# Three pairs of up blocks (13, 16, 19) in two by two steps in the second half, in place of 13 and 17

## The chip, the cores and the metric

The kernel runs on one core of a Trainium2 chip. The metric is the device time of one execution in microseconds, as the median of several runs. The engines go by short names in the profile: PE is TensorE (matrix products), PEld its weight loads, DVE is VectorE, ACT is ScalarE, POOL is GpSimd, SP is SyncE, which here only issues DMAs.

## What is computed

One layer of a residual network on a sequence of 512 positions with 1024 channels: an input projection with a short gated convolution and a causal attention, a gated merge, and then a channel mixer. The change lies in the mixer:

```python
h = rms_norm(x, norm_ffn_g[l])
up = causal_dwconv(h @ w_up[l], conv_ffn_w[l])
a, b = jnp.split(up, 2, axis=-1)
x = x + (jax.nn.silu(a) * b) @ w_down[l]
return rms_norm(x, norm_f_g)
```

`w_up` has 2 x 2816 columns. The causal convolution has three taps along the sequence, with weights of its own for each channel.

## The kernel before

**Layout.** Activations lie with channels on the 128 partitions and the 512 positions along the free axis, cut into two halves of 256. Every product is kept near float32 by splitting both factors into a high part of a shorter type and the rest: wh·xh + wl·xh + wh·xl (`mm3`, `passes`), three matmuls of 128x256 for each half.

**Weight chunks.** All weights come as one list of chunks (`stream`, L176 to L198), in the order of use. For each chunk SyncE's queue loads a raw tile (`load`, L223; five buffers, `NRAW`), ScalarE writes the high part (L281), VectorE the rest (L285); high and low parts have two buffers each (L271). This is `split`. A chunk is split about one chunk ahead of its matmuls.

**Plain and two by two blocks.** Each of the 22 up blocks `j` gives a tile of `a` and one of `b`. I number the chunks `up2j` and `up2j+1` as blocks, and `j` as pair. In a plain pair (`block`, L971) each of the two is 8 x 3 x 2 = 48 matmuls. A pair named in `UPS` goes through `up_pair` (L1090) instead: two output tiles, two input tiles and two position halves make a two by two product, done with seven products where eight would be needed (`PROD`, L343). Such a pair takes its weights as two P chunks (the blocks themselves, 768 columns used) and two F chunks (sums of blocks, 1024 columns), 84 matmuls in all, into four PSUM banks, and five VectorE steps and one of ScalarE put the results together (L1100 to L1106). The forms of the activations that it needs (`tfh`, `tfl`) lie in the buffer `xf`.

**After a pair.** The tile is scaled by the norm (L1124, L1122), convolved (`taps`: one ScalarE step L617, two VectorE taps L618 and L621), `a` goes through silu (L1134) and the product a·b is made on GpSimd (L1137 for even `j`, L1144 for odd). Up to the last pair of `UPS` the scaling is done in place in PSUM; behind it, in the buffer `xg`, which takes over the place of `xf` and also receives the residual from DRAM (L1111).

**Work for the down product.** The down projection is done with the same seven products. For each odd `j` the four forms t1 to t4 (L1154 to L1159) and the high and low parts gh, gl (L1163, L1164) are put on a list `later` with a due chunk and a planned cost. `run_later` (L226) takes them off when a chunk is split, as long as a budget lasts: 1.7 us for an up chunk, 0.45 us for the P and F chunks of an up pair (L291), and it stops at the first due entry that doesn't fit. `glu` empties the list (`flush`, L1139) at the next odd `j`. `after_split` queues what is taken off behind that chunk's split on its engine.

**Sums of weights.** The F chunks are made on the way by DMAs in DRAM (`group`, L134): for each group of two chunks SyncE issues a copy, GpSimd an accumulating add, and this three times, each step resting on the one before. The list `todo` holds them in batches; within a batch the steps of its groups alternate. `ticks` (L245) says how many steps go out when a chunk is split.

**Order.** TensorE's, SyncE's and GpSimd's work around the change is pinned to program order (`keep`). On VectorE and ScalarE, program order is the preference, but an instruction whose inputs are ready may be placed ahead of one whose inputs aren't, when the program is built; the chip then runs each engine in that order.

Of the kernel before, what the change touches and what calls it, by code (L numbers as in the profile page):

```python
# [40 lines left out]
PHASES = ((0, 12), (12, NP))  # L41
# [11 lines left out]
)  # L53
GS = 2
NFF = len(STEPS[0]) + len(STEPS[1])
UPS = (3, 7, 13, 17)
NUP = NFF + 2 * (8 - GS)

PLAIN = [(m, k) for m in (6, 7) for k in range(*PHASES[1])]
PCUTS = (0, 4, 12, 20)  # L60
# [3 lines left out]
def block_kernel(ctx, tc, xT, vecs, wv, win, wmix, wo, wup, wst, wdp, outT):  # L64
# [53 lines left out]
    dsp = ctx.enter_context(tc.tile_pool(name="dsp", bufs=1, space=bass.MemoryType.DRAM))  # L118
    sums = {}
    groups = [[NFF + 2 * j, NFF + 2 * j + 1] for j in range(KB - GS)]  # L120
    ends = [0, 4, len(groups)]
    for (j0, j1), n0, n1 in zip(PHASES, (0, len(STEPS[0])), (len(STEPS[0]), NFF - 1)):
        groups += [[NUP + 2 * i, NUP + 2 * i + 1] for i, j in enumerate(UPS) if j0 <= j < j1]
        if j0:
            ends.append(len(groups))
        groups += [list(range(n, min(n + 2, n1))) for n in range(n0, n1, 2)]
        if not j0:
            ends += [ends[-1] + 4, len(groups)]
    groups.append([NFF - 1])
    ends += [len(groups) - 2, len(groups)]  # L130
    nstep = [len(d) for d in STEPS[0] + STEPS[1]] + [2] * (2 * (KB - GS) + 2 * len(UPS))
    todo = []

# [22 lines left out]
            add(f(6, 8), w(4, 6)),  # L156
        ]

    for i0, i1 in zip(ends, ends[1:]):
        todo += [op for ops in zip(*map(group, range(i0, i1))) for op in ops]  # L160

    def tick():
        if todo:
# [6 lines left out]
    def up_n(j):  # L170
        return [NUP + 2 * UPS.index(j) + d for d in range(2)]

# [13 lines left out]
    n = 0  # L186
    for ph, (j0, j1) in enumerate(PHASES):
        for j in range(j0, j1):
            if j in UPS:
                for m in up_n(j):  # L190
# [35 lines left out]
    def run_later(k, us):  # L226

        n = 0
        while n < len(later):
            if later[n][0] <= k and later[n][1] <= us + 0.1:  # L230
                us -= later[n][1]
                with after_split():
                    later.pop(n)[3]()
            elif later[n][0] <= k:
                return
            else:
                n += 1
# [7 lines left out]
    def ticks(nm):  # L245

        if nm[0] in "iw":
            return 1
        if nm[0] == "m":
            return 2  # L250
        if nm[0] == "u":
            n = int(nm[2:])
            return 2 if (n % 4 == 0 and n > 4) or (n >= 2 * PHASES[1][0] and n % 4 < 3) else 1
        return int(nm[0] == "F" and (int(nm[1:]) % 2 == 1 or int(nm[1:]) >= NUP))

    def split(hl=None):
# [6 lines left out]
        if k >= gs0:  # L263
            for _ in range(ticks(nm)):
                tick()
# [24 lines left out]
        parts.append((hi, lo))  # L290
        run_later(k, 0.45 if nm[0] in "PF" and int(nm[1:]) >= NUP else {"u": 1.7, "P": 1.6, "F": 0.75, "d": 0}.get(nm[0], 3.5))  # L291

# [445 lines left out]
    n = 4 * H  # L738
# [72 lines left out]
    n = len(units)  # L811
# [278 lines left out]
    def up_pair(j):  # L1090

        nonlocal xg, x1
        flush([("xf", q) for q in range(4)])
        p23, p45, p16, p7 = banks = [acc(f"us{j}{i}") for i in range(4)]
        pair(up_n(j), x1_form, banks)
        z = fp.tile([P, S], F32, tag="fu", name=f"uz{j}", bufs=3)
        u = fp.tile([P, S], F32, tag="fu", name=f"uu{j}", bufs=3)[:, : S // 2]
        lo, hi = halves
        with after_split():
            nc.scalar.activation(z[:, lo], p16[:, lo], AF.Copy)  # L1100
            nc.vector.tensor_add(z[:, hi], p16[:, hi], z[:, lo])
            nc.vector.tensor_add(u, p7[:, lo], z[:, hi])
            nc.vector.tensor_add(z[:, hi], p45[:, hi], z[:, hi])
            nc.vector.tensor_add(p23, p23, z)
            p45h = p45.rearrange(halves_of, h=2)
            nc.vector.tensor_add(p45h, p45h, u.unsqueeze(1).to_broadcast([P, 2, S // 2]))  # L1106
        if j == UPS[-1]:
            xg = xfp.tile([P, 4 * KB, 2 * P], F32, tag="xf", name="xg")
            x1 = xg[:, : 2 * KB].rearrange(whole, h=2)
            for a in range(0, KB, 4):  # L1110
                nc.gpsimd.dma_start(x1[:, a : a + 4, :], x1d[:, a : a + 4, :])  # L1111
        return p23, p45

    def up(j, rb2, pu=None):
        uu = []
        if j in UPS:
            pu = up_pair(j)
# [401 lines left out]
```

## Time and profile before

| | us |
|---|---|
| median of 3 runs | 692.53 |
| lowest, highest | 691.62, 692.86 |
| profiled execution | 691.91 |
| its span, first to last instruction | 690.1 |
| first half's up blocks, from the first matmul of block 0 | 338.30 |
| first half's down steps | 466.68 to 523.80 |
| second half's up blocks | 523.80 to 629.92 |
| second half's down steps | 629.92 to 665.62 |

The lower rows are places in the profiled execution, in us from its span's start, read from the chain of work that ended last. Rows of engines give the start, the length, the engine, the line of the kernel, the operation, the tiles (out<-in) and in brackets how long the engine stood idle before, and who ended it. In rows of stages, the busy time of PE, PEld, DVE, ACT and POOL follow each other with their counts, then TensorE's granted clock, the DMA share and GB/s.

### The profile page before, as it was taken

How to read it: one execution, taken by the hardware profiler on the slowest of the kernel's cores; microseconds unless marked ns; L12 is line 12 of the kernel's file. 1: busy time of each engine (PE TensorE's matmuls, PEld its weight loads, DVE VectorE, ACT ScalarE, POOL GpSimd, SP SyncE). 2: the span in 40 equal slices, each digit the busy share in tenths (PEclk: the TensorE clock that was granted, in tenths of full speed). 3: DMA queues.
4: the chain of work that ended last, by engine and by line, in shares of the span. 5: the costliest groups of instructions: out<-in, count | busy, mean ns of one | idle time of the engine just before them, and what ended most of it. 6: DMA issues, size and time to landing. Idle time of an engine off the chain costs nothing.

```text
span 690.1 us, 14688 instructions
## 1 busy us (share of the span) xinstructions
PE 681.7 (99%) x5928; PEld 679.9 (99%) x5928; DVE 542.5 (79%) x857; ACT 362.2 (52%) x578; POOL 182.3 (26%) x206
## 2 busy tenths in 40 slices
PE   9999999999999999999999999999999999999995
PEld 9999999999999999999999999999999999999995
DVE  6678777886687877768887988977665897988785
ACT  6575556554564544446654536545433455535663
POOL 5123745444021010233412123330122134230000
PEclk9999999999999999999999999999999999999998
DMA  8526957478489696878696768679799978753523
GB/s 308 196 86 218 204 148 172 102 185 168 127 224 284 208 266 186 250 248 268 202 201 172 181 161 232 149 175 229 218 300 301 277 175 214 233 162 119 178 77 122
DMA packets 64196, 136.75 MB, mean 198 GB/s; under 512 B 5728, under 2 KB 29280, under 8 KB 63872
## 3 DMA queue, kind: packets, MB, share of 16 engines
q1 hardware_dynamic: 43488, 103.89, 45.7%
q0 software_dynamic: 19920, 31.23, 25.9%
q8 instruction: 46, 0.75, 0.4%
q10 hardware_dynamic: 720, 0.69, 0.3%
q14 instruction: 22, 0.18, 0.1%
HBM read 129.44 MB, written 47.71 MB: 257 GB/s over the span
## 4 chain that ended last, share of the span: by engine, by line
PE 95%; DVE 2%; ACT 1%; issue 1%; ACTq 0%; DVEq 0%
PE p_up L314 22%; PE p_in L314 14%; PE dn L332 13%; PE gs L332 8%; PE p_up L332 7%; PE p_wo L314 6%; PE us L332 6%; PE yc L332 3%; PE ya L314 3%; PE pa L526 2%; PE pb L528 2%; PE p_g L314 2%; PE o L707 2%; PE tp L692 1%; PE pdB L314 1%; PE pdA L314 1%
## 5 line engine op out<-in xcount | busy, mean ns | idle before, releaser
L314 PE MATMUL p_in<-xf,wh_in 128*128 128x256 f32 x576 | 95.7, 278 | 0.0
L148 POOL DMA_DIRECT2D sum<-in_wst_dram x63 | 66.0, 1180 | 112.4 <-DMA sum<-sum 83.5
L314 PE MATMUL p_up<-x1h,wl_up 128*128 128x256 f32 x440 | 85.7, 276 | 0.0
L314 PE MATMUL p_up<-x1l,wh_up 128*128 128x256 f32 x440 | 85.7, 276 | 0.0
L314 PE MATMUL p_up<-x1h,wh_up 128*128 128x256 f32 x440 | 85.7, 276 | 0.0
L314 PEld LDWEIGHTS p_in<-xf,wh_in 128*128 128x128 f32 x576 | 80.4, 188 | 0.7
L281 ACT ACTIVATE wh_F<-raw_F 128x1024 fp32r<-128x1024 f32 (+1 forms) x40 | 42.0, 1051 | 63.6 <-PE ya L314 25.8
L285 DVE TENSOR_TENSOR wl_F<-raw_F,wh_F 128x1024 fp32r<-128x1024 f32 (+1 forms) x40 | 50.2, 1256 | 27.8 <-ACT wh_F L281 26.6
L314 PEld LDWEIGHTS p_up<-x1h,wl_up 128*128 128x128 f32 x440 | 66.3, 188 | 0.0
L314 PEld LDWEIGHTS p_up<-x1l,wh_up 128*128 128x128 f32 x440 | 66.2, 188 | 0.0
L314 PEld LDWEIGHTS p_up<-x1h,wh_up 128*128 128x128 f32 x440 | 66.2, 188 | 0.0
L314 PE MATMUL p_in<-xf,wl_in 128*128 128x256 f32 x288 | 56.6, 278 | 0.1
L285 DVE TENSOR_TENSOR wl_up<-raw_up,wh_up 128x1024 fp32r<-128x1024 f32 x36 | 44.7, 1242 | 11.6 <-ACT wh_up L281 11.5
L281 ACT ACTIVATE wh_P<-raw_P 128x768 fp32r<-128x768 f32 (+1 forms) x40 | 33.4, 834 | 38.5 <-PE p_up L314 16.8
L281 ACT ACTIVATE wh_up<-raw_up 128x1024 fp32r<-128x1024 f32 x36 | 38.0, 1055 | 25.5 <-PE p_up L314 16.6
L285 DVE TENSOR_TENSOR wl_P<-raw_P,wh_P 128x768 fp32r<-128x768 f32 (+1 forms) x40 | 38.3, 956 | 11.6 <-ACT wh_P L281 6.2
L314 PEld LDWEIGHTS p_in<-xf,wl_in 128*128 128x128 f32 x288 | 43.5, 188 | 0.3 <-DVE wl_in L285 0.3
L1137 POOL TENSOR_TENSOR ge<-fu,fu 128x512 f32<-128x512 f32 x11 | 22.2, 2015 | 72.4 <-DVE fu L621 49.1
L332 PE MATMUL dn<-gl,wh_F 128*128 128x256 f32 x156 | 36.4, 276 | 0.0
L332 PE MATMUL dn<-gh,wh_F 128*128 128x256 f32 x156 | 36.3, 276 | 0.0
L285 DVE TENSOR_TENSOR wl_in<-raw_in,wh_in 128x1024 fp32r<-128x1024 f32 x24 | 30.2, 1256 | 6.1 <-ACT wh_in L281 6.0
L332 PE MATMUL p_up<-x1h,wh_up 128*128 128x256 f32 x136 | 32.5, 276 | 0.0
(361 smaller groups left out, 2074.8 us busy)
## 6 DMA issues: line engine op xcount, KB each, us to landing
raw_F<-sum SPq DMA_DIRECT2D x39, 512.0 KB, 5.9
raw_up<-in_wup_dram SPq DMA_DIRECT2D x36, 512.0 KB, 4.1
raw_P<-in_wst_dram SPq DMA_DIRECT2D x39, 384.0 KB, 3.8
raw_in<-in_win_dram SPq DMA_DIRECT2D x24, 512.0 KB, 3.7
sum<-in_wst_dram POOLq DMA_DIRECT2D x39, 256.0 KB, 6.4
sum<-in_wst_dram SPq DMA_DIRECT2D x19, 512.0 KB, 8.2
sum<-in_wst_dram POOLq DMA_DIRECT2D x19, 512.0 KB, 8.4
sum<-sum SPq DMA_DIRECT2D x38, 256.0 KB, 4.1
```

The source lines that it names most:

```text
L148: return lambda: keep(nc.gpsimd.dma_start(dst, src, accum_op=ALU.add))
L281: ins = nc.scalar.activation(hi, raw, AF.Copy)
L285: ins = nc.vector.tensor_sub(lo, raw, hi.bitcast(F32))
L314: keep(nc.tensor.matmul(out[:, cs], w, x[:, cs], start=start and i == 0 and c == 0, stop=stop and i == 2 and c == len(cut) - 1,))
L332: keep(nc.tensor.matmul(out, wl if x == 1 else wh, xl if x == 2 else xh, start=opens and bk not in seen, stop=closes and bk not in left,))
L526: keep(nc.tensor.matmul(pa[t][:, :VW], xt, w[:, :VW], start=start, stop=stop))
L528: keep(nc.tensor.matmul(pb[t], xt, w[:, VW:], start=start and t % 2 == 0, stop=stop and t % 2 == 1))
L692: keep(nc.tensor.transpose(tp[:, ks], pt[:, ks], ident))
L707: keep(nc.tensor.matmul(o[:, os_], vv[:, kb, pr, e, :], x[:, kb, cs], start=e == 0 and kb == 0 and i == 0, stop=e == 1 and kb == nk - 1 an ...
L1137: keep(nc.gpsimd.tensor_mul(ge, a.rearrange(halves_of, h=2), b.rearrange(halves_of, h=2)))
```

## The change

The second half's pairs in two by two steps are now 13, 16 and 19; 17 becomes a plain pair. That adds one group of weight sums, six DMA steps, to the 126 there were. The batches are written out as a tuple. More steps go out per chunk: two instead of one at wo2, wo4 and wo6 and at up10, up18 and up22. Since the scaling in PSUM goes up to the last pair of `UPS`, blocks 36 to 39 are now scaled there too, and the load of the residual follows pair 19.

```diff
-UPS = (3, 7, 13, 17)
+UPS = (3, 7, 13, 16, 19)
 NUP = NFF + 2 * (8 - GS)
+MIXED = (4, 2, 4, 4, 2, 4, 2)
...
     groups = [[NFF + 2 * j, NFF + 2 * j + 1] for j in range(KB - GS)]
-    ends = [0, 4, len(groups)]
     for (j0, j1), n0, n1 in zip(PHASES, (0, len(STEPS[0])), (len(STEPS[0]), NFF - 1)):
         groups += [[NUP + 2 * i, NUP + 2 * i + 1] for i, j in enumerate(UPS) if j0 <= j < j1]
-        if j0:
-            ends.append(len(groups))
         groups += [list(range(n, min(n + 2, n1))) for n in range(n0, n1, 2)]
-        if not j0:
-            ends += [ends[-1] + 4, len(groups)]
     groups.append([NFF - 1])
-    ends += [len(groups) - 2, len(groups)]
...
-    for i0, i1 in zip(ends, ends[1:]):
-        todo += [op for ops in zip(*map(group, range(i0, i1))) for op in ops]
+    i0 = 0
+    for n in MIXED:
+        todo += [op for ops in zip(*map(group, range(i0, i0 + n))) for op in ops]
+        i0 += n
+    assert i0 == len(groups)
...
         if nm[0] in "iw":
-            return 1
+            return 2 if nm in ("wo2", "wo4", "wo6") else 1
...
         if nm[0] == "u":
             n = int(nm[2:])
-            return 2 if (n % 4 == 0 and n > 4) or (n >= 2 * PHASES[1][0] and n % 4 < 3) else 1
+            return 2 if n > 4 and n % (4 if n >= 2 * PHASES[1][0] else 2) != (3 if n >= 2 * PHASES[1][0] else 1) else 1
```

Before, the batches held 4, 2, 4, 4, 2, 3 and 2 groups; now 4, 2, 4, 4, 2, 4 and 2, and the one group of pair 19 leads the sixth.

## The prediction

> **What bounds the kernel now.** I read the page first (shares of busy time, chain of work that ended last), then the chain in order of time around one pair of up blocks, then the busy time by stage, and last the order of VectorE's instructions there.
>
> ```profile
> span 690.1 us, 14688 instructions
> PE 681.7 (99%) x5928; PEld 679.9 (99%) x5928; DVE 542.5 (79%) x857; ACT 362.2 (52%) x578; POOL 182.3 (26%) x206
> PE 95%; DVE 2%; ACT 1%; issue 1%; ACTq 0%; DVEq 0%
> ```
>
> TensorE carries 95% of the chain and is never far from busy. A shorter list of matmuls is worth its full time, as long as nothing else takes TensorE's place. The chain in order of time (start, length, what, matmuls) shows the pace:
>
> ```profile
> 565.96 1.36 PE p_up L332 x12
> 567.32 4.08 PE p_up L314 x36
> ...
> 576.84 9.57 PE us L332 x84
> 586.40 1.36 PE p_up L332 x12
> ...
> 597.28 1.36 PE p_up L332 x12
> ```
>
> A plain block is 48 matmuls in 1.36 + 4.08 = 5.44 us, so 0.1133 us each, and blocks follow without a gap. A pair in two by two steps (the rows "us") is 84 matmuls: 84 x 0.1133 = 9.52, and pair 17 took 9.57, so 0.05 us was lost in it. Next, who is close behind TensorE: the stages between pair 13 and the down steps (us, then busy time per engine).
>
> ```profile
> 534.68:544.20 9.52, 9.52 (x86) 9.52 (x86) 7.49 (x7) 5.37 (x6) 1.43 (x2) 1.00 1.08 281
> 544.20:576.84 32.64, 32.64 (x290) 32.64 (x290) 29.38 (x44) 13.91 (x21) 11.02 (x9) 1.00 0.74 192
> 576.84:586.40 9.56, 9.56 (x86) 9.56 (x86) 7.54 (x10) 7.32 (x11) 3.80 (x3) 1.00 1.02 267
> 586.40:629.92 43.52, 43.52 (x387) 43.52 (x386) 39.67 (x60) 21.30 (x32) 12.09 (x10) 1.00 0.59 176
> ```
>
> The third column of busy times is VectorE: 7.49 + 29.38 + 7.54 + 39.67 = 84.08 of 95.24 us, 88%. It is the second bound of just this stage. ScalarE and GpSimd have room (47.90 and 28.34 by the same sums).
>
> **The change part by part. TensorE:** pair 19 becomes a two by two pair, 2 x 5.44 = 10.88 us out, 9.52 in: **-1.36 us**. Pair 16 takes the place of pair 17, which moves work and saves nothing. That is the whole gain, 0.20% of 692.53.
>
> **VectorE's sum.** Four splits for a pair in place of two, five combining steps more; the groups of splits by line (count | busy, mean ns | idle before, and its causes),
>
> ```profile
> L285 DVE TENSOR_TENSOR wl_up<-raw_up,wh_up 128x1024 fp32r<-128x1024 f32 x36 | 44.7, 1242 | 11.6 <-ACT wh_up L281 11.5
> L285 DVE TENSOR_TENSOR wl_F<-raw_F,wh_F 128x1024 fp32r<-128x1024 f32 (+1 forms) x40 | 50.2, 1256 | 27.8 <-ACT wh_F L281 26.6 <-DMA raw_up<-in_wup_dram 0.9 <-issue 0.2
> L285 DVE TENSOR_TENSOR wl_P<-raw_P,wh_P 128x768 fp32r<-128x768 f32 (+1 forms) x40 | 38.3, 956 | 11.6 <-ACT wh_P L281 6.2 <-PE gs L332 5.5
> ```
>
> and VectorE's instructions around pair 17's end in order of time (start, length):
>
> ```profile
> 584.14 1.25 DVE L285 TENSOR_TENSOR wl_up<-raw_up,wh_up 128x1024 fp32r<-128x1024 f32 x1 [0.99 <-ACT wh_up L281]
> 585.30 0.68 DVE L1164 TENSOR_TENSOR gl<-ge,gh 128x512 fp32r<-128x512 f32 x1
> 585.91 1.89 DVE L1164 TENSOR_TENSOR gl<-go,gh 128x512 fp32r<-128x512 f32 x3
> 587.72 0.41 DVE L1101 TENSOR_TENSOR uz<-us,uz 128x256 f32<-128x256 f32 x1
> 588.05 1.21 DVE L285 TENSOR_TENSOR wl_up<-raw_up,wh_up 128x1024 fp32r<-128x1024 f32 x1
> ...
> 591.29 0.69 DVE L1124 TENSOR_TENSOR us<-us,rb_n 128x512 f32<-128x512 f32 x1
> 591.89 0.69 DVE L1122 SCALAR_TENSOR_TENSOR us<-us,rb_n 128x512 f32<-128x512 f32 x1
> 592.49 0.68 DVE L1124 TENSOR_TENSOR xg<-p_up,rb_n 128x512 f32<-128x512 f32 x1
> 593.09 0.74 DVE L618 SCALAR_TENSOR_TENSOR fu<-us,vec,fu 128x511 f32<-128x511 f32 x1
> 593.75 1.23 DVE L285 TENSOR_TENSOR wl_up<-raw_up,wh_up 128x1024 fp32r<-128x1024 f32 x1
> 594.89 0.74 DVE L621 SCALAR_TENSOR_TENSOR fu<-us,vec,fu 128x510 f32<-128x510 f32 x1
> ...
> 601.96 1.21 DVE L285 TENSOR_TENSOR wl_up<-raw_up,wh_up 128x1024 fp32r<-128x1024 f32 x1
> ```
>
> Splits: 2 x 0.956 + 2 x 1.256 - 2 x 1.242 = 1.94 us. Combining runs from 587.72 to 591.29 with one split of 1.14 in it: 2.4 us. The stage then asks 84.08 + 4.3 = 88.4 us of VectorE in 95.24 - 1.36 = 93.9 us, 94%. On average it fits; the question is where the work falls. From start to start, in these rows, a multiply costs 0.60, a tap 0.66, a split 1.14 and a step of gl 0.60 (585.30 to 587.72 is 2.42 for four).
>
> **VectorE's deadline.** Pair 16 is followed by blocks 34, 35, 36 as pair 17 was by 36, 37, 38. A block's first eight matmuls (12 in the chain's piece, of which four are the low part) need only the high half; the low half must be there 8 x 0.1133 = 0.91 us after the block's start. For the third block after a split that began at 584.14, that is 597.28 + 0.91 = 598.19: **14.05 us**. What stands ahead of that split in program order, in before: two splits and itself 3.42, gl of pair 15 2.42, combining 2.4, three multiplies 1.80, six taps 3.96: 14.0 us. It fitted with nothing to spare. Program order didn't decide, though: the split at 593.75 overtook five taps and ended at 594.98, 3.2 us early. Its successor of 601.96 ended 603.17, against 597.28 + 5.44 + 0.91 = 603.63: 0.46 us in hand.
>
> After the change there is one thing more in that window. Pair 15's steps t1 to t4 (0.85 us by the planner's costs, twice) ran here, in a hole between plain blocks:
>
> ```profile
> 570.21 0.42 DVE L1154 TENSOR_TENSOR go<-ge 128x256 f32<-128x256 f32 x1
> ...
> 572.76 0.43 DVE L1155 TENSOR_TENSOR go<-go,ge 128x256 f32<-128x256 f32 x1 [1.48 <-POOL go L1144]
> 573.10 0.42 DVE L1158 SCALAR_TENSOR_TENSOR go<-go 128x256 f32<-128x256 f32 x1
> 573.56 0.42 DVE L1159 SCALAR_TENSOR_TENSOR go<-go 128x256 f32<-128x256 f32 x1
> 573.90 0.69 DVE L1124 TENSOR_TENSOR p_up<-p_up,rb_n 128x512 f32<-128x512 f32 x1
> ```
>
> The last three take 573.90 - 572.76 = 1.14 from start to start, the first another 0.34: 1.5 us. Pair 16 now begins where block 32 did (565.96), and its four chunks allow 0.45 us each, which 0.85 exceeds, so they wait for block 34: 14.0 + 1.5 = 15.5 us for 14.05, **1.4 us late**. Two of the four gl steps also come only when pair 17's product flushes the list, behind block 35's evacuation (0.60 + 2 x 0.66 = 1.92 more): 3.4 late at worst. At best the split overtakes as it did in before and the cost is 0. I take **2.2**, between 1.4 and 3.4, since the gl steps now lie ready in the hole that the split used at 593.75.
>
> **ScalarE at pair 16's first F chunk.** The F chunk is needed 18 x 0.1133 = 2.04 us into the pair. ScalarE's order at pair 17:
>
> ```profile
> 576.99 0.63 ACT L1134 ACTIVATE fu<-fu 128x512 f32<-128x512 f32 x1 [1.67 <-DVE fu L621]
> 577.52 1.04 ACT L281 ACTIVATE wh_F<-raw_F 128x1024 fp32r<-128x1024 f32 x1
> ```
>
> In before a silu that waited for VectorE stood ahead of it, and it ended at 577.52 + 1.04 = 578.56 for 576.84 + 2.04 = 578.88. With pair 15's silu in that place, and VectorE later by up to 1 us, it costs 0 to 1.2 us; I take 0.3, near the 0.05 that pair 17 lost.
>
> **Rest of the stage.** Time that VectorE stands idle inside a pair is no use to it, since the next chunk's buffer isn't free: 9.52 - 7.49 = 2.03 us in pair 13, 9.56 - 7.54 = 2.02 in pair 17. Three times that, 6.1 us, is more than the 93.9 - 88.4 = 5.5 left, so VectorE stays behind into the down steps: 0.6 us by this sum, 0 if the holes are filled, 2 if a pair's idle time is lost once more. I take 0.7.
>
> **Costed at nothing.** Scaling blocks 36 to 39 in PSUM rather than in xg (0.69 against 0.68 in the rows above). The load of x1 now follows pair 19; its first use in the sums of the down steps is some 40 us later, so I find no bill for it, 2 us of ScalarE at most if its copy of x1 waits. DMA and GpSimd: one group more is three copies and three adds, and pair 19 loads two P and two F chunks for two up chunks. First the adds as a group, then one row of GpSimd's order near the end of the output projection, the longest DMA time of the sums, and SyncE's wait for them (us in total, times, longest):
>
> ```profile
> L148 POOL DMA_DIRECT2D sum<-in_wst_dram x63 | 66.0, 1180 | 112.4 <-DMA sum<-sum 83.5 <-DMA sum<-in_wst_dram 28.6 <-issue 0.2
> ```
>
> ```profile
> 337.23 0.56 POOL L1021 DMA_DIRECT2D x1d<-xr  x1 [4.51 <-DVE xr L1015]
> ```
>
> ```profile
> sum<-in_wst_dram POOLq DMA_DIRECT2D x19, 512.0 KB, 8.4
> ```
>
> ```profile
> SPq L145 <- DMA sum<-in_wst_dram: 88.1, 21, 10.6
> ```
>
> 3 x 1.18 = 3.5 us of GpSimd fit its idle time. SyncE's queue stood up to 10.6 us behind one copy with weights queued after it, and in the split rows above only 0.9 us of VectorE's idle time ended with a weight load. Six more steps go out from wo2 to up22, so the steps for pair 19 end six chunks before its first F load. The first adds of the third batch now fall into wo6 and wo7, in GpSimd's queue ahead of the last x1 stores and square sums, on which the second norm waits: two adds, 2.4 us, against the 4.51 us that GpSimd idled there (0 to 2.4 if their copies land late; I take 0). Five buffers of 5.44 us cover a stop of 10.6; uncovered, it costs 0 to 4 us.
>
> [...] GpSimd and VectorE meet here, in the order of time of each:
>
> ```profile
> 539.46 1.29 POOL L1137 TENSOR_TENSOR ge<-fu,fu 128x512 f32<-128x512 f32 x1 [4.63 <-DVE fu L621]
> ```
>
> ```profile
> 539.66 2.16 DVE L285 TENSOR_TENSOR wl_F<-raw_F,wh_F 128x1024 fp32r<-128x1024 f32 x1 [0.44 <-ACT wh_F L281]
> ```
>
> The split took 2.16 instead of 1.23 us beside the product. [...]
>
> **The sum:** -1.36 + 2.2 + 0.3 + 0.7 = **+1.84 us** if all terms fall due; since a stall at block 36 lets VectorE catch up and takes from the last term, I forecast **+1.5 us**. The profiled execution took 691.91 (span 690.1), 0.62 under the median of 692.53; I add to the median: **694.0 us**.
>
> **Rivals. (a) VectorE's order hides all** (not slower): the split of block 36 overtakes, as its like did at 593.75. The second window then has these 1.5 us more, but pair 17's own t steps, which lay ahead of the split of 601.96, now follow it, so about 0.46 stays in hand: 692.53 - 1.36 = 691.2. For it: the overtaking in before; against: 94% load. **(b) VectorE in debt to the end:** 3.4 + 1.2 + 2.0 - 1.36 = +5.2: 697.7. For it: 100% busy stretches follow every pair. **(c) A stop of SyncE's queue** late in the ups: +2 after the saving: 694.5; against: 0.59 DMA share in the last stage. That fewer matmuls aren't issued at all can't be: the chunks of pair 19 say so.
>
> **How the numbers follow.** Forecast 0.46 (692.3 to 695.8), (a) 0.28, (b) 0.16, (c) 0.10. About 0.2%, 1.39 us, is what can be told from no change. Faster needs all of (a) and a little luck, half of it: 0.14. Slower is above 693.9: half the forecast, (b) and most of (c): 0.46. Same: 0.40. The range, 691.0 to 696.8, takes in (a) and leaves out the far ends of (b).
>
> **What would show it.** In the profile after: pair 19 as 84 matmuls in 9.5 us; a gap of 1.4 to 3.4 us in TensorE at block 36, the third after pair 16, ended by wl_up; t1 to t4 of pair 15 behind block 34's split. A chain without gaps would prove (a); a wait of wh or wl for a weight load, (c).

## The result and the profile after

| | before | after |
|---|---|---|
| median, us (10 runs each, taken together) | 692.38 | 694.96 |
| lowest, highest | 691.62, 693.76 | 693.45, 695.38 |
| profiled execution, and its span | 691.91, 690.1 | 693.69, 691.9 |

The ratio after to before is 1.0033, with a 95% interval of 1.0023 to 1.0042: the change costs 2.6 us by the medians. In the kernel after, helper lines stand two lower: the split is L279 and L283, matmuls are L312 and L330, the multiplies L1122 and L1120, the taps L616 and L619, t1 to t4 L1152 to L1157, gl L1162, silu L1132. The kernels of the experiments have line numbers of their own; there, go by the tiles. The page, first lines and chain:

```profile
span 691.9 us, 14692 instructions
PE 681.3 (98%) x5916; PEld 678.7 (98%) x5916; DVE 548.3 (79%) x864; ACT 364.5 (53%) x581; POOL 184.6 (27%) x209
PE 86%; DVE 8%; ACT 3%; issue 2%; DMA 1%; ACTq 0%; SPq 0%; DVEq 0%
```

Twelve matmuls fewer, as costed, and still TensorE's share of the chain fell from 95% to 86%: VectorE now carries 8%. The chain in order of time shows where it does, and that pair 19 runs at full pace:

```profile
589.25 1.14 DVE wl_up L283
590.43 0.75 PE p_up L330 x4
591.18 4.08 PE p_up L312 x36
...
600.70 9.52 PE us L330 x84
...
626.54 1.60 PE p_up L330 x12
...
632.31 1.37 PE dn L330 x12
633.69 1.05 ACT wh_F L279
634.79 33.95 PE dn L330 x297
668.74 6.80 PE pdA L312 x60
```

TensorE's waits by what ended them (us in total, times, longest):

```profile
PE p_up L330 <- DVE wl_up L283: 2.7, 1, 2.7
...
PE dn L330 <- ACT wh_F L279: 0.4, 1, 0.4
...
PE us L330 <- ACT wh_F L279: 0.2, 1, 0.2
```

The wait shown is less than what it costs, since the rows of matmuls overlap (0.28 us long here, 0.1133 from start to start). I measure the cost from start to start, less 0.1133 us for each matmul between. At block 36:

```profile
587.50 0.28 PE L330 MATMUL p_up<-x1l,wh_up 128*128 128x256 f32 x1
590.43 0.75 PE L330 MATMUL p_up<-x1h,wl_up 128*128 128x256 f32 x4 [2.65 <-DVE wl_up L283]
591.02 0.39 PE L312 MATMUL p_up<-x1h,wh_up 128*128 128x256 f32 x2
```

From 587.50 to 591.02 are 3.52 us for five matmuls, which take 0.57 at full pace: **2.95 us lost**. In the same way pair 16's first F chunk lost 0.45, block 43 0.25, and the first F chunk of the down steps 0.71; in before the up blocks and the down steps of the second half lost 0.05 in all. The sum is 4.36.

The books of the two profiled executions: the up blocks of the second half took 632.31 - 523.84 = 108.47 us against 106.12, that is +2.35 (= -1.36 + 0.45 + 2.95 + 0.25, and 0.06 in small pieces). The down steps took 36.43 against 35.70, +0.73. The rest, from the plain products to the end of the span, took 691.9 - 668.74 = 23.2 against 24.5, **-1.3**, which nobody had planned. Together +1.8, the difference of the spans. The medians differ by 2.6, though: of after's ten times, two lie at 693.45 and 693.69 (the profiled one) and eight at 694.85 to 695.38. So there are three things to explain: the gaps, the shorter end, and the second group of times.

### The profile page after: what moved, and what is told of

It is laid out like the page before. It is cut to its first block, busy times and chain, and to the rows that moved or that the text cites. A ratio compares the mean times of both kernels' runs of the same rounds, so it can differ in the third digit from the quotient of the medians.

```text
span 691.9 us, 14692 instructions
## 1 busy us (share of the span) xinstructions
PE 681.3 (98%) x5916; PEld 678.7 (98%) x5916; DVE 548.3 (79%) x864; ACT 364.5 (53%) x581; POOL 184.6 (27%) x209
## 4 chain that ended last, share of the span: by engine, by line
PE 86%; DVE 8%; ACT 3%; issue 2%; DMA 1%; ACTq 0%; SPq 0%; DVEq 0%
PE p_up L312 17%; PE p_in L312 14%; PE dn L330 13%; PE gs L330 8%; PE p_wo L312 6%; PE us L330 6%; PE p_up L330 5%; PE yc L330 3%; PE ya L312 3%; PE o L705 2%; PE pa L524 2%; PE pb L526 1%; PE tp L690 1%; PE pdB L312 1%; PE pdA L312 1%
## 5 line engine op out<-in xcount | busy, mean ns | idle before, releaser
L143 POOL DMA_DIRECT2D sum<-in_wst_dram x66 | 70.9, 1227 | 96.1 <-DMA sum<-sum 67.6
L312 PE MATMUL p_in<-xf,wh_in 128*128 128x256 f32 x576 | 95.7, 278 | 0.0
L312 PE MATMUL p_up<-x1h,wh_up 128*128 128x256 f32 x416 | 81.1, 276 | 0.0
L312 PEld LDWEIGHTS p_in<-xf,wh_in 128*128 128x128 f32 x576 | 80.4, 188 | 0.7
L312 PE MATMUL p_up<-x1h,wl_up 128*128 128x256 f32 x416 | 81.0, 276 | 0.0
L312 PE MATMUL p_up<-x1l,wh_up 128*128 128x256 f32 x416 | 81.0, 276 | 0.0
L279 ACT ACTIVATE wh_F<-raw_F 128x1024 fp32r<-128x1024 f32 (+1 forms) x42 | 44.2, 1052 | 65.0 <-PE ya L312 25.8
L283 DVE TENSOR_TENSOR wl_F<-raw_F,wh_F 128x1024 fp32r<-128x1024 f32 (+1 forms) x42 | 53.5, 1275 | 28.6 <-ACT wh_F L279 28.3
L312 PEld LDWEIGHTS p_up<-x1h,wh_up 128*128 128x128 f32 x416 | 62.7, 188 | 0.0
L312 PEld LDWEIGHTS p_up<-x1h,wl_up 128*128 128x128 f32 x416 | 62.6, 188 | 0.0
L312 PEld LDWEIGHTS p_up<-x1l,wh_up 128*128 128x128 f32 x416 | 62.6, 188 | 0.0
L312 PE MATMUL p_in<-xf,wl_in 128*128 128x256 f32 x288 | 56.6, 278 | 0.1
L279 ACT ACTIVATE wh_P<-raw_P 128x768 fp32r<-128x768 f32 (+1 forms) x42 | 35.1, 836 | 39.6 <-PE p_up L312 17.9
L279 ACT ACTIVATE wh_up<-raw_up 128x1024 fp32r<-128x1024 f32 x34 | 35.9, 1057 | 28.6 <-PE p_up L312 14.1
L283 DVE TENSOR_TENSOR wl_up<-raw_up,wh_up 128x1024 fp32r<-128x1024 f32 x34 | 42.3, 1244 | 9.5 <-ACT wh_up L279 9.4
L283 DVE TENSOR_TENSOR wl_P<-raw_P,wh_P 128x768 fp32r<-128x768 f32 (+1 forms) x42 | 40.1, 956 | 11.5 <-ACT wh_P L279 6.0
L312 PEld LDWEIGHTS p_in<-xf,wl_in 128*128 128x128 f32 x288 | 43.6, 188 | 0.3 <-DVE wl_in L283 0.3
L330 PE MATMUL dn<-gh,wh_F 128*128 128x256 f32 x156 | 36.5, 277 | 0.4 <-ACT wh_F L279 0.4
L330 PE MATMUL dn<-gl,wh_F 128*128 128x256 f32 x156 | 36.4, 276 | 0.0
L283 DVE TENSOR_TENSOR wl_in<-raw_in,wh_in 128x1024 fp32r<-128x1024 f32 x24 | 30.2, 1257 | 6.1 <-ACT wh_in L279 3.4
L1142 POOL TENSOR_TENSOR go<-fu,fu 128x512 f32<-128x512 f32 x9 | 12.6, 1396 | 72.9 <-DVE fu L619 54.5
```

Of the source, the lines that this page charges most:

```text
L143: return lambda: keep(nc.gpsimd.dma_start(dst, src, accum_op=ALU.add))
L279: ins = nc.scalar.activation(hi, raw, AF.Copy)
L283: ins = nc.vector.tensor_sub(lo, raw, hi.bitcast(F32))
L312: keep(nc.tensor.matmul(out[:, cs], w, x[:, cs], start=start and i == 0 and c == 0, stop=stop and i == 2 and c == len(cut) - 1,))
L330: keep(nc.tensor.matmul(out, wl if x == 1 else wh, xl if x == 2 else xh, start=opens and bk not in seen, stop=closes and bk not in left,))
L1142: return eng.tensor_mul(go[:, 0:2, :], a.rearrange(halves_of, h=2), b.rearrange(halves_of, h=2))
```

## The experiments

**1. The same kernel once more.**

> The kernel after once more, unchanged, for a second profile and more times. Of ten times two lay at 693.5 to 693.7 and eight at 694.9 to 695.4, and the profiled execution was one of the two. Theory (a gap of 2.7 us sometimes lets TensorE's granted clock fall, as the profiles of the denser schedule and of pair 16 in place of 17 showed behind gaps of 2.9 and 1.9 us): the times fall into the same two groups, and if the profiled execution is one of the upper group, its matmuls behind block 36's gap take 0.21 us in place of 0.113 for some 2.5 to 3 us, 1.2 to 1.7 us in all. Rival (the upper group has another cause, as a DMA that lands late): an upper execution shows full clock and a longer or a second gap.

Times 693.33 and 693.37, and 694.51 to 696.84 (four); 1.0039 of before, 1.0023 to 1.0054. The profiled execution, 694.71, was of the upper group. TensorE there, in order of time:

```profile
587.43 0.28 PE L330 MATMUL p_up<-x1l,wh_up 128*128 128x256 f32 x1
590.36 1.22 PE L330 MATMUL p_up<-x1h,wl_up 128*128 128x256 f32 x4 [2.65 <-DVE wl_up L283]
591.38 0.63 PE L312 MATMUL p_up<-x1h,wh_up 128*128 128x256 f32 x2
591.81 0.63 PE L312 MATMUL p_up<-x1h,wl_up 128*128 128x256 f32 x2
```

The gap is the same to the hundredth. Behind it two matmuls take 0.43 us (591.38 to 591.81) in place of 0.23, until 593.4. That is 1.3 us more, and the table by stage gives a granted clock of 0.68 for 590 to 595, where the first profile had 1.00. So the stall at block 36 is paid twice in most executions of this kernel: once as the wait (2.65 us), and once as the slow stretch behind it (1.3 us). The mean granted clock of the executions agrees: in the sixteen of both sets it is 0.997 to 0.998 in the four of the lower group and 0.994 to 0.996 in the other twelve. That explains the second group, but for the one time of 696.84, which lies 1.6 us above the others of its set.

**2. Pair 15's work earlier.** The last F chunk of pair 16 gets the budget of an up chunk, so t1 to t4 and gl of pair 15 don't wait for block 34.

```diff
-        run_later(k, 0.45 if ...
+        run_later(k, 1.7 if nm == f"F{NUP + 7}" else 0.45 if ...
```

> The kernel after, with the budget at the last F chunk of pair 16 at 1.7 us in place of 0.45, so that t1 to t4 of pair 15 (1.5 us) and its gl steps run inside pair 16 rather than behind block 34's split. Theory (the 1.5 us of t1 to t4 are what the window to block 36 could not take): the gap at block 36 is gone or under 0.5 us, the time about 692.3 (691.5 to 693.2). Rival 1 (VectorE's load, not this work's place): the gap stays at 2 us or more. Rival 2 (the work only moves): the gap goes and another of 1 us or more appears at blocks 34 or 35, whose splits now stand behind this work; time 693.5 to 695.

Median 691.47, ratio to before 0.9991 (0.9981 to 1.0001): 3.5 us under after by the medians, 2.9 by the two ratios to before. The gap at block 36 is gone; the losses at the first F chunks of pairs 16 and 19 and of the down steps and one at block 42 stay, 1.9 us in all. VectorE's order says why. First the kernel after, from block 34's split to block 36's:

```profile
573.72 1.25 DVE L283 TENSOR_TENSOR wl_up<-raw_up,wh_up 128x1024 fp32r<-128x1024 f32 x1 [0.98 <-ACT wh_up L279]
574.90 0.41 DVE L1152 TENSOR_TENSOR go<-ge 128x256 f32<-128x256 f32 x1
...
576.02 0.42 DVE L1157 SCALAR_TENSOR_TENSOR go<-go 128x256 f32<-128x256 f32 x1
576.36 1.22 DVE L283 TENSOR_TENSOR wl_up<-raw_up,wh_up 128x1024 fp32r<-128x1024 f32 x1
...
585.91 0.74 DVE L616 SCALAR_TENSOR_TENSOR fu<-p_up,vec,fu 128x511 f32<-128x511 f32 x1
586.57 1.42 DVE L1162 TENSOR_TENSOR gl<-go,gh 128x512 fp32r<-128x512 f32 x1
587.91 0.74 DVE L619 SCALAR_TENSOR_TENSOR fu<-p_up,vec,fu 128x510 f32<-128x510 f32 x1
588.57 0.68 DVE L1122 TENSOR_TENSOR p_up<-p_up,rb_n 128x512 f32<-128x512 f32 x1
589.16 1.21 DVE L283 TENSOR_TENSOR wl_up<-raw_up,wh_up 128x1024 fp32r<-128x1024 f32 x1
```

Then the kernel with the earlier budget, the same split of block 36:

```profile
574.06 0.41 DVE L1153 TENSOR_TENSOR go<-go,ge 128x256 f32<-128x256 f32 x1
...
583.98 1.21 DVE L283 TENSOR_TENSOR wl_up<-raw_up,wh_up 128x1024 fp32r<-128x1024 f32 x1
585.11 1.40 DVE L616 SCALAR_TENSOR_TENSOR fu<-us,vec,fu 128x511 f32<-128x511 f32 x2
```

In after the split comes at 589.16, behind six taps, the last gl and block 35's multiply. With t1 to t4 and the gl steps of pair 15 out of the way (1.5 us and one late gl) it comes at 583.98, ahead of the taps, as its like did at 593.75 before the change: 5.2 us earlier for some 3 us of work moved, since the split now overtakes.

**3. The splits placed ahead.**

```diff
             p = pu[s_] if pu else block(f"up{2 * j + s_}", x1h, x1l, True)
+            if j == 17 and len(parts) == chunk.n:
+                split()
```

> The kernel after, with one thing moved: in pair 17 the splits of blocks 35 and 36 are called ahead of the evacuations of blocks 34 and 35, so that in VectorE's order the split of block 36 stands ahead of the taps of pair 17. Theory (the split of block 36 stands too far back in VectorE's order): the gap of 2.7 us at block 36 is gone or under 0.5, VectorE's busy time in the stage is the same, and the time falls by 2 to 2.9 us to about 692.3. Rival (VectorE simply has too much to do behind pair 16, whatever its order): the gap goes to one of blocks 37 to 39 or to pair 19, in sum over 2 us, and the time stays at 694.5 to 695.

Median 693.89, ratio 1.0023 (1.0012 to 1.0035). Both theories hit and missed: blocks 34 to 37 run without a gap, but 2.49 us are now lost at block 42, the third after pair 19. VectorE's order there repeats the picture of block 36:

```profile
605.10 1.22 DVE L283 TENSOR_TENSOR wl_up<-raw_up,wh_up 128x1024 fp32r<-128x1024 f32 x1 [0.19 <-ACT wh_up L279]
606.24 0.42 DVE L1154 TENSOR_TENSOR go<-ge 128x256 f32<-128x256 f32 x1
...
614.63 1.21 DVE L283 TENSOR_TENSOR wl_up<-raw_up,wh_up 128x1024 fp32r<-128x1024 f32 x1
```

The t steps and gl of pair 17 now fall behind pair 19's first split. So the argument of the window holds there too, and a gap avoided at one pair was handed to the next.

**4. Pair 16 in place of 17, without a third pair** (`UPS = (3, 7, 13, 16)` in the kernel before).

> Before with pair 16 in two by two steps in place of 17, and no third pair: the number of matmuls is that of before. Theory (the stall comes from pair 16's place, right behind an odd plain pair): the gap of 2 to 3 us at block 36 and the one of 0.2 to 0.4 at pair 16's first F chunk are there as in the kernel after, and the time is 2.3 to 3.4 us over before, about 695.2. Rival (the debt of three pairs is what stalls): no gap over 0.5 us at block 36, time within 0.6 us of before.

Median 696.25, ratio 1.0053 (1.0040 to 1.0065). The place alone does it, without a third pair: 0.43 us at pair 16's first F chunk, 2.25 at block 36, and then a slow stretch of 1.7 us, in sum 4.4, with no matmul saved. I had not counted the slow stretch. VectorE just ahead of block 36's split:

```profile
586.55 0.69 DVE L1164 TENSOR_TENSOR gl<-go,gh 128x512 fp32r<-128x512 f32 x1
587.15 0.74 DVE L621 SCALAR_TENSOR_TENSOR fu<-xg,vec,fu 128x510 f32<-128x510 f32 x1
...
588.41 1.21 DVE L285 TENSOR_TENSOR wl_up<-raw_up,wh_up 128x1024 fp32r<-128x1024 f32 x1
```

It is the order of after, 0.75 us earlier, and all of that is one row: gl takes 0.60 from start to start here and 1.34 in after, where GpSimd made its product at the same time (in experiment 4 it made it only at 592.79):

```profile
586.15 1.29 POOL L1135 TENSOR_TENSOR ge<-fu,fu 128x512 f32<-128x512 f32 x1 [9.13 <-ACT fu L1132]
```

**5. Only the schedule of the sums** (after, with the pairs of before).

```diff
-UPS = (3, 7, 13, 16, 19)
+UPS = (3, 7, 13, 17)
-MIXED = (4, 2, 4, 4, 2, 4, 2)
+MIXED = (4, 2, 4, 4, 2, 3, 2)
```

> The pairs of before (13 and 17) with the batches and the steps per chunk of after: only the schedule of the sums of weights is that of the change. Theory (these DMAs cost nothing): within 0.4 us of before, 692.0 to 692.8, and TensorE without a gap over 0.3 us in the second half's up blocks. Rival (part of the loss comes from the denser sums): 0.6 us or more over before, with a wait on a DMA or on GpSimd behind wo2 to wo7 or up10, up18, up22.

Median 696.64, ratio 1.0062 (1.0043 to 1.0080): a clear miss. ScalarE and GpSimd behind pair 17:

```profile
594.09 0.72 ACT L615 ACTIVATE fu<-xg,vec 128x512 f32<-128x512 f32 x1
600.65 0.42 ACT L1343 ACTIVATE gh<-xg 128x256 fp32r<-128x256 f32 x1 [5.84 <-DMA xg<-x1d]
600.97 0.62 ACT L1132 ACTIVATE fu<-fu 128x512 f32<-128x512 f32 x1
```

```profile
588.67 0.81 POOL L143 DMA_DIRECT2D sum<-in_wst_dram  x1 [3.67 <-DMA sum<-sum]
589.19 1.44 POOL L1109 DMA_DIRECT2D xg<-x1d  x2
```

The load of x1 stands in GpSimd's queue behind an add that waited 3.67 us for its copy; before the change it went out at 586.71, here at 589.19. ScalarE has a small copy of x1 (L1343) in its order right behind pair 17, and stands at it for 5.84 us, against 1.97 in before, with pair 17's silu behind it. The same two rows in before:

```profile
586.71 1.16 POOL L1111 DMA_DIRECT2D xg<-x1d  x2 [0.75 <-PE us L332]
```

```profile
596.88 0.42 ACT L1345 ACTIVATE gh<-xg 128x256 fp32r<-128x256 f32 x1 [1.97 <-DMA xg<-x1d]
```

In the kernel with the denser sums a gap of 2.94 us at block 39 follows, and a slow stretch of 2.7 us.

**6. The same, with x1's copy late.** Only one of the last products uses the copy, some 80 us later (596.88 to 675.83 in before); the planner had put it early since it reckoned x1 to be there.

```diff
-    nc.scalar.activation(xlast[0], y7, AF.Copy)
-    nc.vector.tensor_sub(xlast[1], y7, xlast[0].bitcast(F32))
+    with after_split():
+        nc.scalar.activation(xlast[0], y7, AF.Copy)
+        nc.vector.tensor_sub(xlast[1], y7, xlast[0].bitcast(F32))
```

> The pairs of before with the schedule of sums of after, and the copy of x1 moved back in ScalarE's order to where it is used. With the copy early this schedule took 696.6. Theory (the denser sums cost only because x1 lands later and ScalarE stands at its copy, 5.8 us): no gap over 0.3 us in the second half's up blocks, full clock, 691.8 to 692.6 like before. Rival (the sums take something else, such as the transfers of weights): 694 or more, with the gap at block 39 still there and another wait ahead of it.

Median 691.58, ratio 0.9994 (0.9985 to 1.0003), without a gap behind pair 17. So the denser sums themselves cost nothing in the up blocks. The time isn't quite like before's for another reason: this kernel has the shorter end of experiment 9 (4.8 us for 5.9), and its last products come 0.3 us later. The price of the copy is therefore better taken against before, whose median in the set of experiment 5 was 691.93: one instruction of 0.42 us in a wrong place had cost 4.7 us.

**7. The same step on top of experiment 2.**

> The kernel with the budget of 1.7 us at pair 16's last F chunk, and besides it the copy of x1 that stands in ScalarE's order behind pair 19, 60 us before its use, moved back to where it is used. Theory (ScalarE stands 2.3 us at that copy until x1 has landed, and silu and the high parts behind it are late): ScalarE's wait for x1 goes, the gap of 0.38 us at block 42 shrinks or goes, and the gap at the first down step (0.78 us) too in part; 0.3 to 0.9 us under the kernel without this, about 690.9. Rival (VectorE alone is late there): the same gaps, time within 0.2 us of 691.5.

Median 691.49 (0.9995, 0.9986 to 1.0004) against 691.47: a miss. ScalarE's wait for x1 is gone and the loss at block 42 falls from 0.38 to under 0.2 us, but the down steps reach their first F chunk at 632.17 in both kernels. So with pair 19 last, that wait (2.53 us in after) costs nothing that shows.

**8. ScalarE's order at the F chunks.** In after, ScalarE at pair 16 and at the down steps:

```profile
566.58 0.64 ACT L1132 ACTIVATE fu<-fu 128x512 f32<-128x512 f32 x1 [3.25 <-DVE fu L619]
567.12 1.05 ACT L279 ACTIVATE wh_F<-raw_F 128x1024 fp32r<-128x1024 f32 x1
```

```profile
633.15 0.64 ACT L1132 ACTIVATE fu<-fu 128x512 f32<-128x512 f32 x1 [3.23 <-DVE fu L619]
633.69 1.04 ACT L279 ACTIVATE wh_F<-raw_F 128x1024 fp32r<-128x1024 f32 x1
```

ScalarE idles for a tap of VectorE with the high part queued behind. On top of experiment 7, the splits are called ahead of silu there, and silu is put behind them; the sum steps stay where they were, by lines that are left out here.

```diff
...
+        if j + 1 in (*UPS[-2:], PHASES[1][1]):
+            if j % 2:
+                flush()
+            split(now=False)
+            split(now=False)
+            with after_split():
+                nc.scalar.activation(a, a, AF.Silu)
+        else:
+            nc.scalar.activation(a, a, AF.Silu)
```

> The kernel with pair 15's work early and x1's copy late, and besides it ScalarE's high parts of the first F chunk of pair 16, of pair 19 and of the down steps ahead of the silu that waited for VectorE's tap there; VectorE's order is unchanged. Theory (what is left of the loss are these three places: 0.43, 0.27 and 0.71 us against the pace of 0.1133 us per matmul): all three under 0.1, time 1.2 to 1.5 us under the kernel without this, about 690.1. Rival (VectorE's low parts or the later products then stall TensorE at the blocks behind): two or more gaps of 0.3 us elsewhere, time 691 or more.

Median 689.91, ratio to before **0.9967 (0.9956 to 0.9978)**: faster than both kernels, by 2.2 and 5 us. ScalarE and the chain now:

```profile
565.95 1.06 ACT L284 ACTIVATE wh_F<-raw_F 128x1024 fp32r<-128x1024 f32 x1 [2.76 <-PE p_up L317]
...
567.64 0.62 ACT L1143 ACTIVATE fu<-fu 128x512 f32<-128x512 f32 x1
```

```profile
565.87 9.52 PE us L335 x84
...
624.01 0.74 PE p_up L335 x4
...
628.83 35.26 PE dn L335 x311
```

The high part starts with the pair, and the three places are free of loss. VectorE's 864 instructions stand in the same order as in experiment 7, and of ScalarE's 581 only the three silu steps moved, so ScalarE's order alone was the cause there. Only block 42 still loses 0.41, to the low part that VectorE made at 622.75. Of the 2.2 us under before, 1.3 are the shorter end (4.6 us for 5.9, see experiment 9), and TensorE's part is 1.36 - 0.41 = 0.95.

**9. The shorter end.** From the issue of the last output copies to the end of the span it is 5.9 us in before (684.22 to 690.1) and 4.6 in after (687.34 to 691.9). Three kernels, each the one before with something idle added: five copies on SyncE's queue, six small copies on VectorE, six on ScalarE.

> Before with five short copies more on SyncE's queue (their data is not used), as many DMAs as the third pair brings there. From the issue of the last output copies to the end of the span it is 5.9 us in all kernels with two pairs, 4.6 in all with three, and the queue of instruction loads shows 22 loads against 23. Theory (the shorter end comes from where SyncE's program is loaded, not from the third pair's work): the end is 4.6 us, 23 loads, and the time is 1.0 to 1.4 us under before, about 690.8. Rival (the end depends on the work or its data): 5.9 us, time as before or up to 0.5 over it.

> Before with six copies of one column on VectorE more (their data is not used). Five copies more on SyncE's queue had left the end of the span at 5.7 us behind the issue of the last output copies. In all runs so far the end is 5.7 to 5.9 us where VectorE's program has 1090 instructions and ScalarE's at most 847, and 4.6 to 4.8 where VectorE's has 1091 or more and ScalarE's 848 or more. Theory (VectorE's program length decides, by where its last load of instructions falls): the end is 4.6 to 4.8 us, the time 0.8 to 1.3 us under before, about 691.0. Rival (ScalarE's): 5.7 to 5.9 us, time as before.

> Before with six copies of one column on ScalarE more (their data is not used), the counterpart to the six on VectorE. Theory (VectorE's program length decides over the end): 5.7 to 5.9 us from the last issue to the end, time as before or up to 0.3 over it. Rival (ScalarE's does): 4.6 to 4.8 us, 0.8 to 1.3 under before. If both kernels have the long end, neither length is the cause.

The copies on SyncE's queue changed nothing: 5.7 us, 1.0008 (0.9999 to 1.0017). The times of the other two can't be compared with before. They took 703.01 and 703.82 (1.0158 and 1.0169), with no wait that accounts for it: both have a new tile of 24 bytes per partition, and a block took 1.42 + 4.25 = 5.67 us for 5.44. Their ends can be compared with each other, though, since their matmuls end within 0.04 us: with the six on VectorE the end is 5.2 us (696.02 to 701.2), with the six on ScalarE 6.0 (696.06 to 702.1). That speaks for VectorE's program and against ScalarE's. Hence once more, with six copies of an old tile onto itself:

```diff
+            if j == 5:
+                with after_split():
+                    for i in range(6):
+                        nc.vector.tensor_copy(tbl, tbl)
```

> Before with six copies more on VectorE again, this time of a small tile onto itself, so that no new tile moves the others in SBUF (with a new tile of 24 bytes per partition each matmul took 0.1163 us in place of 0.1133, and the question of the end was not answered). Theory (the length of VectorE's program, 1096 instructions for 1090, decides where its last instructions are loaded): matmuls at 0.1133 us, the end 4.6 to 4.8 us behind the issue of the last output copies in place of 5.9, time 0.8 to 1.3 us under before, about 691.0. Rival (it has another cause): the end is 5.7 to 5.9 us, time as before or up to 0.3 over it; then the cause of the shorter end stays open.

Median 691.05, ratio 0.9990 (0.9981 to 0.9999). The issue of the last copies, in before and in this kernel, whose spans are 690.1 and 689.2:

```profile
684.22 1.63 ACTq L1383 DMA_DIRECT2D out_dram<-xg  x2
```

```profile
684.36 1.63 ACTq L1387 DMA_DIRECT2D out_dram<-xg  x2
```

The end is 4.8 us for 5.9, with six instructions that do nothing. The change brings VectorE eight more (1098 for 1090, counted in the trace), and the end with them. All fourteen profiles fall in line: 5.7 to 6.0 us with 1090 instructions on VectorE, 4.8 to 5.2 with 1091 or 1096, and 4.6 with 1098 or more. That the end goes with the length of VectorE's program is shown by these; that it works through the loading of its last instructions is a guess of mine that no run shows. The count of loads that I had named doesn't follow: it stays at 22 here and is 23 in after.

## Why the prediction was right

The forecast was +1.5 us and slower, +2.6 came, inside the range. Point by point:

- **TensorE, -1.36:** right. Pair 19 is 84 matmuls in 9.52 us.
- **VectorE's sum, 88.4 us:** right. The stages from pair 13 to the down steps in the table by stage (sum of us, then busy time per engine) give 88.31:

```profile
sum 97.59, PE 94.76 PEld 94.21 DVE 88.31 ACT 49.22 POOL 29.91; mean PE 15.79 PEld 15.70 DVE 14.72 ACT 8.20 POOL 4.99
```

- **The deadline at block 36:** the mechanism was right and the size short, 2.2 against 2.95. From 573.72 to the split's end at 590.37 VectorE worked without a hole for 16.65 us. Counted were 15.5; block 35's multiply (588.57) adds 0.6, as part of the worst case had it, and the one slow gl 0.74, together 0.2 more than measured. Of the two gl steps that the worst case had behind the rest, one came late. The prediction has a split that took 2.16 us beside a product of GpSimd; here it was a gl step that took longer, 1.34 us from start to start beside the product and 0.60 without it (the rows of experiment 4). Why it takes longer there is not shown.
- **ScalarE at pair 16's first F chunk:** right, 0.45 for 0.3, and shown by experiment 8. The working gave the chunk more room than it had: in before its first matmul stands at 578.72, not 578.88, so the high part was 0.16 us early and not 0.32.
- **The rest of the stage, 0.7:** the size fits (0.25 at block 43 and 0.71 at the down steps), the reason only in part. The larger piece, the 0.71, was no debt of VectorE's as such but the same order on ScalarE as at pair 16, and went when that order changed while VectorE's stayed (experiment 8).
- **The discount of 0.34,** since a stall lets VectorE catch up: wrong. Nothing came back; the four losses add up to 4.36 where the terms had 3.2.
- **Costed at nothing:** the sums are free, as said, but "its first use in the sums of the down steps is some 40 us later" was wrong for x1. ScalarE's order holds a copy of it right behind the last pair, and the trace of before showed that wait (1.97 us). In after it costs nothing; with the old pairs the same schedule cost 4.7 us through it.
- **Not seen at all:** the slow stretch behind the gap, +1.3 in most executions, and the shorter end, -1.3. They cancel. Without them the terms that were counted come to -1.36 + 4.36 = +3.0. So the sign rests on the reasons given; that the number came as near as it did is partly luck.

Rival (a) fell, since the split did not overtake; in experiment 2, with pair 15's steps out of its way, it did. Rival (b) put the loss at 6.6 us, 4.4 came. Rival (c) left no wait in after.

## What to carry to other kernels

Where one engine is at its bound and another close behind it, like VectorE's 94% here, look for the window between two deadlines and add up what falls into it; an average that fits says little. When work is moved, follow it to where its planner puts it next, and look in every engine's order for an instruction that waits for something far off while urgent work is queued behind it. Before a change is given up, move what stalls: the pairs that lost 2.6 us gain 2.2 with three orders changed, 1.3 of it from the shorter end.

## What was not expected of the hardware

- **TensorE was slower behind a short stall.** Gaps of 1.95, 2.65 and 2.94 us (experiments 4, 1 and 5) were followed by matmuls of 0.213 us in place of 0.113 for 3 to 6 us, at a cost of 1.7, 1.3 and 2.7 us; the granted clock was 0.68 for 590 to 595 in experiment 1, and 0.58 for 605 to 610 and 0.74 for 610 to 615 in experiment 5. The same 2.65 us were followed by a granted clock of 1.00 in the first profile of after. What decides between the two is not shown.
- **A new small tile.** One tile of 24 bytes more per partition made a plain block 4% slower, 5.67 for 5.44 us, in both kernels that had it, at a granted clock of 0.997; six copies without it left the pace as it was. The second half's down steps kept their pace beside it (315 matmuls in 35.71 us, 35.70 before), so not all matmuls were slower. That the new tile moved others in SBUF and that their places are the cause is a guess of mine that no run shows.
- **The length of a program.** Six idle instructions on VectorE shortened the end by 1.0 us. Measured against before with these six (691.05), the best kernel's 689.91 is 1.1 us better, of the 1.36 that fewer matmuls could bring.
